# Four adaLN products per weight step kept side by side on TensorE, in the order 2, 3, 0, 1

## The chip, the cores and the metric

One core of a Trainium2 chip (trn2) runs the program. The metric is the device time of one execution in microseconds (us), and what is compared is the median of several executions.

## The reference, cut to what matters

One inference step of a two-layer backbone. 1024 sample tokens and 128 prompt tokens of width 1024 go through the same trunk: a convolutional mixer and a feed-forward in layer 0, attention and a feed-forward in layer 1. Each layer is steered by six vectors, computed from a conditioning vector, one for the samples and one for the prompt:

```
mod = silu(cond) @ ada_w[i] + ada_b[i]             # ada_w[i] is 1024 x 6144, cond 1 x 1024
sh1, sc1, g1, sh2, sc2, g2 = split(mod, 6)
h = modulate(rmsnorm(x, norm1_g[i]), sh1, sc1)
y = conformer_conv(h, ...)  or  gqa_mixer(h, ...)
x = x + g1 * y
h = modulate(rmsnorm(x, norm2_g[i]), sh2, sc2)
x = x + g2 * conv_ffn(h, ...)
```

`conformer_conv` is a product with 2 x 1024 columns, a gate `a * sigmoid(g)`, a depthwise convolution of 31 taps over the tokens, a layer norm, silu, and a product with 1024 columns.

## The kernel before

All 1152 tokens stay in SBUF with features on the partitions, in three chunks of 384 columns. Every large product is made of three (`mm3`, L245 to L249): weights and activations are split into a high and a low part, and high x high, high x low and low x high are summed. A weight tile of 128 x 1024 numbers is loaded by `Weights.load` (L209), split on ScalarE and VectorE (L220, L221) and handed out by `take`; loads run up to three tiles ahead.

The adaLN vectors come from `ada` (L252 to L303). A group is 2048 columns of `ada_w`; there are six groups, three for each layer. A group runs over the 1024 rows of `ada_w` in eight steps of 128 rows. For a step, `load` (L253) issues two transfers of 128 x 1024 numbers, half 0 and half 1 of the columns, each into a buffer of the tag `adaw`. The step then has four products (L270): the conditioning vectors (128 x 32, `cs`) against 512 columns each, products 0 and 1 on half 0, products 2 and 3 on half 1. Product q writes PSUM partitions 32q to 32q+31, so each of the four uses its own strip of 32 columns of TensorE. The next step's two loads are issued before this step's products stand in the program. After eight steps ScalarE copies the sums into a row that also takes an `adaw` buffer (L279), TensorE transposes it (L283), and VectorE adds the bias (L287).

The first group runs at the start, with seven `adaw` buffers. The other five run beside the convolution (L679): `ada` is a generator in the list `bg`, and every call of `tick` moves it by one step. For this the phase gives `adaw` three buffers (L633):

```
sC, slot_c = phase(adaw=(3, D), pacc=(2, CONV_N), tmp=(2, CONV_N))
```

The convolution's first product, `gated` (L572 to L600), goes over eight tiles j of 128 features. A tile takes two weight tiles, and for each of the three chunks computes `ppa` and `ppg`, 24 products of 384 columns each, so 144 products for a tile; then ScalarE takes the sigmoid (L594) and VectorE multiplies (L597). There are three ticks in a chunk, nine in a tile. With the taps behind it, VectorE does 19 (L658, L660) and GpSimd the rest (L651). Of the last tile, 16 taps are products with diagonals on TensorE (`dl`, L706); the mean of the layer norm is taken by products (`mu`, L722, L726). The layer norm and the product `pw2` follow.

What sets the order of the work. The whole program stands in `manual_schedule(engines={SP})`: the SP queue issues all these transfers in the order in which they are written, so weight loads and adaLN loads share one line. On the other engines the order is planned when the program is built (`schedule_with_timeline_sim=True`): the planner walks through its own estimate of time, and of the instructions whose inputs are there by that estimate the one written earliest goes first. The engines then run their lists in that order. A region under `manual_schedule(engines=ATT_ENGINES)`, which is TensorE alone, keeps the written order of its TensorE instructions; in the kernel before, only the attention of layer 1 is such a region.

Of the kernel before, what the change touches and what calls it, by code (L numbers as in the profile page):

```python
# [13 lines left out]
PSUM = bass.MemoryType.PSUM  # L14
# [4 lines left out]
KT = D // P  # L19
# [29 lines left out]
ATT_ENGINES = {mybir.EngineType.PE}  # L49
# [16 lines left out]


def pieces(c):
    """A chunk's columns by the conditioning of their tokens."""
    lo, hi = c * CH, (c + 1) * CH  # L70
    out = []
    if lo < NS:
        out.append((0, min(hi, NS) - lo, 0))
    if hi > NS:
        out.append((max(lo, NS) - lo, CH, 1))
    return out
# [3 lines left out]
def tile_hybrid_step(ctx: ExitStack, tc: tile.TileContext, a: dict, outs: list):  # L80
    nc = tc.nc
# [14 lines left out]
        return xp.tile([P, KT, CH], F32, tag="x", name=name)  # L96

    def phase(**slots):
        """SBUF of a phase: so many tiles of so many columns for each tag."""
        stack = ExitStack()  # L100
        pools = {
            tag: (stack.enter_context(tc.tile_pool(name=f"s_{tag}", bufs=bufs, reuse_waits="tile")), n)
            for tag, (bufs, n) in slots.items()
        }

        def tile_(tag, name, dt=F32, n=None):
            pool_, cols_ = pools[tag]
            return pool_.tile([P, n or cols_], dt, tag=tag, name=name)

        return stack, tile_  # L110
# [13 lines left out]
        return hh, hl  # L124

    class Banks:
        """PSUM, cut anew for some phases."""

        stack = None

# [12 lines left out]

    pool = Banks()

    # work that runs beside the products, a step after each of them
    bg = []

    def tick():
# [18 lines left out]

    xs_d = [dp.tile([P, NCH, KT, CH], F32, name=f"xs_d{i}") for i in range(2)]

    # ---- weights, in the order of their use: loads run up to three tiles ahead, the split into hi + lo (both exact
    # in float32r) one or two ----
    def ffn_order(l):
        up = a["ffn_w_up"][l]
        down_at = dict(DOWN)
# [23 lines left out]
    class Weights:  # L199
# [22 lines left out]
            self.ready[i] = tuple(t.rearrange("p (k n) -> p k n", n=n) if n else t for t in (hi, lo))  # L222

        def ahead(self, splits, loads):
            """Has everything up to so many tiles from the next one split or loaded."""
            for i in range(self.at, min(self.at + max(splits, loads), len(self.order))):
                if self.order[i][0] == "stop":
                    break
                if i < self.at + loads and i not in self.raw and i not in self.ready:
                    self.load(i)  # L230
                if i < self.at + splits and i not in self.ready:
                    self.split(i)
# [10 lines left out]
    weights = Weights()  # L243
# [4 lines left out]
        nc.tensor.matmul(ps, wh, ml, start=False, stop=False)  # L248
        nc.tensor.matmul(ps, wl, mh, start=False, stop=last)  # L249

# [1 line left out]
    def ada(pool, l, grp):  # L252
        def load(kt):  # L253
            out = []
            for half in range(2):
                w = slot("adaw", f"adaw{l}_{grp}_{kt}_{half}")
                c0 = grp * 2048 + half * 1024
                nc.sync.dma_start(w, a["ada_w"][l, kt * P : (kt + 1) * P, c0 : c0 + 1024])
                out.append(w)
            return out  # L260

        nxt = load(0)
        yield
        ps = pool("ms", f"ada{l}_{grp}")
        for kt in range(KT):
            w = nxt
            if kt + 1 < KT:
                nxt = load(kt + 1)
            for q in range(4):
                nc.tensor.matmul(  # L270
                    ps[32 * q : 32 * q + 32, :],
                    cs[:, kt, :],
                    w[q // 2][:, (q % 2) * 512 : (q % 2) * 512 + 512],
                    start=(kt == 0),
                    stop=(kt == KT - 1),
                )
            yield
        row = slot("adaw", f"adar{l}_{grp}", n=512)
        nc.scalar.activation(row, ps, AF.Copy)  # L279
        yield  # L280
        pt = pool("ms", f"adat{l}_{grp}")
        for i in range(4):
            nc.tensor.transpose(pt[:, i * P : (i + 1) * P], row[:, i * P : (i + 1) * P], ident)  # L283
        ptv = pt.rearrange("p (i q c) -> p q i c", i=4, c=32)
        b0 = grp * 16
        for cond in range(2):
            nc.vector.tensor_tensor(  # L287
                mods[l][:, b0 : b0 + 16, cond].rearrange("p (q i) -> p q i", i=4),
                ptv[:, :, :, cond],
                adab[:, l * 48 + b0 : l * 48 + b0 + 16].rearrange("p (q i) -> p q i", i=4),  # L290
                ALU.add,
            )
        for n, gname in ((0, "norm1_g"), (1, "norm2_g")):
            v = 1 + 3 * n
            if v // 2 == grp:
                for cond in range(2):
                    nc.vector.scalar_tensor_tensor(
                        gsc[l][n][:, :, cond],
                        mods[l][:, v * 8 : v * 8 + 8, cond],
                        1.0,  # L300
                        cols(gname, l * KT, KT),
                        ALU.add,
                        ALU.mult,  # L303
                    )
# [1 line left out]
    def mod(l, v, j, cond):  # L306
        return mods[l][:, v * 8 + j, cond : cond + 1]

# [1 line left out]
    def add_stat(acc, j, c, src, eng=None, tag=None):  # L310
        d = acc[:, c * CH : (c + 1) * CH]
        if j == 0:
# [4 lines left out]
            (eng or nc.gpsimd).tensor_tensor(d, d, sq, ALU.add)  # L317

    def token_rstd(pool, parts, name, bank=None):
        """Sums over features of all parts[f, token], then (mean + eps) ** -0.5, tokens on partitions."""  # L320
        n = CH // P
        ps = pool("ms", f"{name}_s") if bank is None else bank[:, CH:]
        for t in range(n):
            for i, x in enumerate(parts):
                nc.tensor.matmul(
                    ps[:, t : t + 1], x[:, t * P : (t + 1) * P], ones, start=(i == 0), stop=(i == len(parts) - 1)
                )
        return rstd_of(ps[:, 0:n], 1.0 / D, n, name)
# [6 lines left out]
        return rs  # L335

    def spread(pool, v, name, bank=None):
        """v[token, t] to every partition, tokens along the columns."""
        n = v.shape[1]
        ps = pool("ms", f"{name}_b") if bank is None else bank  # L340
        for t in range(n):
# [46 lines left out]
        nc.sync.dma_start(t, xs_d[i][:, c])  # L388
        return t

# [1 line left out]
    def ffn(pool, H, X, l, name, beside, done):  # L392
        acts = {}

# [83 lines left out]
        for g in gens:  # L478
            yield from g

    # =========================== layer 0 ===========================
    pool.open(mm=(4, 512), acc=(1, 1536), ms=(1, 512))

# [1 line left out]
    vec_rows = [  # L485
        ("c", a["c"].rearrange("b (r p) -> (b r) p", p=P)),
        ("c_ctx", a["c_ctx"].rearrange("(r p) -> r p", p=P)),
# [32 lines left out]
        nc.sync.dma_start(crow[at[name] : at[name] + KT, :], src)  # L520

    def load_x(c):
        """A chunk's tokens, on partitions, where the low parts of the normed chunks go later."""
        n = CH // P
        toks = hp.tile([P, n, D], F32, tag="hl", name=f"xt{c}")
        for t in range(n):
# [48 lines left out]
        pass  # L575
    weights.ahead(0, RING)

    # conformer: gated pointwise, depthwise over tokens, layernorm, silu, pointwise
    us = []

    def gated(j, c):
        """The products of a chunk; yields before their gating."""
        if c == 0:
            us.append((weights.take(min(j, 1)), weights.take(min(j, 1)), slot("u", f"u{j}")))
            for z in (0, NS + HALF, NT + 2 * HALF):
# [54 lines left out]
        return dww[:, j, t : t + 1]  # L640

    def taps_pool(j, u, pacc, t0, s0_, s1_):
        """The taps from t0 on, with the bias."""
        d = pacc[:, s0_:s1_]
        nc.scalar.activation(
            d, u[:, s0_ + t0 : s1_ + t0], AF.Identity, scale=tap(j, t0), bias=col("conv_dw_b", j)
# [4 lines left out]
            nc.gpsimd.tensor_tensor(d, d, tmp, ALU.add)  # L651

    def taps_vector(j, u, d, n, s0_, s1_, fresh):
        """The first n taps."""
        for t in range(n):
            src = u[:, s0_ + t : s1_ + t]
            if t == 0 and fresh:
# [31 lines left out]
        for c in range(NCH):  # L689
            join(j, da, pacc, c)  # L690

    # the last tile: some taps as products with diagonals, the others on top of them, chunk by chunk, so that the norm
    # of a chunk runs beside the taps of the next
    u = us[last][2]
    t0 = TAPS - POOL_TAPS_7
    te = t0 - PE_TAPS
# [107 lines left out]
    )  # L804
    H = H2

    # =========================== layer 1 ===========================
    # rotary tables with the norm gains folded in, tokens on partitions; gains: plain, halves swapped and signed
    NB = NS // P + 1
    sF.close()  # L810
    sK, slot = phase(s=(4 * NKV, SLOT))
# [55 lines left out]
            put_v(cv[:, kv * P : (kv + 1) * P], kv, NS // P)  # L867

    def head_norm(ps, which, tt, name):
        """RMS norm of two heads, rotary unless they are the prompt's; yields between its stages."""  # L870
        ss = tiny(f"{name}ss", 2)
        for h in range(2):
            nc.scalar.activation(
# [33 lines left out]
        yield xn  # L907

    def place(b, tt, o):
        """Heads to [feature, token]."""  # L910
        pt = pool("t", f"ptqk{b}_{tt}")
        for h in range(2):
            nc.tensor.transpose(pt[:, h * P : (h + 1) * P], o[:, h * P : (h + 1) * P], ident)
# [10 lines left out]
                AF.Copy,  # L924
            )

    # each slot: the products of a tile, then a further stage of each tile before it, the oldest first
    stages = []

    def advance():  # L930
# [46 lines left out]
    GRP = NH // NKV  # L977
    PC, PO = NCH - 1, NS - (NCH - 1) * CH

    # the prompt's queries see the prompt's own keys: the four heads of a group at once  # L980
    def prompt():
        for kv in range(NKV):
            q = qT[PC][:, kv * GRP : (kv + 1) * GRP, PO : PO + P]
# [50 lines left out]
            )  # L1034
            yield

    # samples: blocks of one head and the queries of one chunk, in steps of 128 queries; the scores run two steps
    # ahead of the transposes, the product with V one block behind them
    blocks = [(c, h) for c in range(NCH) for h in range(NH)]
    nq_of = lambda c: CH // P if c < PC else PO // P  # L1040
    steps = [(i, t) for i, (c, h) in enumerate(blocks) for t in range(nq_of(c))]
# [23 lines left out]
        st["ps"].append(ps)  # L1065

    def softmax(s, st):
        """Yields before each part of its exponential."""
        v = st["v"]
        nb, ls, ri = v[:, 3:4], v[:, 4:7], v[:, 7:8]  # L1070
        nc.vector.tensor_reduce(nb, v[:, 0:3], AX.X, ALU.max)
# [117 lines left out]
        project_residual(O, X, c, acc3, 1, "wo", "g")  # L1189
        bg.append(norm_mod(pool, X, acc3, c, 1, 1, H, "n3"))  # L1190

    # final norm, back to tokens on partitions
    gfs = []

    def final(acc, c):
# [40 lines left out]


def _rope_table():
    """cos and sin by position on the 64-wide grid: [128, 2, 9, 32]; block t < 8 is the row part of token tile t,
    block 8 the column part, which all tiles share."""  # L1240
    import numpy as np

    freqs = np.float32(10000.0) ** (-np.arange(0, 64, 2, dtype=np.float32) / np.float32(64))
# [32 lines left out]
```

## Time and profile before

| | before |
|---|---|
| median of 3 runs | 2789.68 us (2787.78 to 2792.02) |
| span of the profiled execution | 2789.3 us |
| PE busy | 2724.6 us, 98% of the span |
| DVE busy | 1585.4 us, 57% |
| ACT busy | 1053.5 us, 38% |
| POOL busy | 699.6 us, 25% |
| adaLN loads | 96 of 512 KB, 4.4 us from issue to landing in the median |

PE is TensorE, PEld its weight loads, DVE VectorE, ACT ScalarE, POOL GpSimd, SP the queue of SyncE that issues the transfers. A row of a timeline gives the start in us from the first instruction, how long the run of like instructions took, the engine, the line of the kernel, what it writes and reads, the shapes, how many instructions (x), and in brackets the idle time before it with what ended it. A product of two f32 operands is recorded as two instructions, so `x4` on an adaLN row is two products and `x8` is four; one with split operands (`ppa`, `ppg`) is one. The profiled execution's own time is told by its span alone; it lies within the three runs and 0.4 us under their median.

### The profile page before, as it was taken

The numbers are of one execution on the slowest core, as the hardware profiler recorded it, in microseconds if no ns is written. First come the engines' busy times: TensorE is split into PE (matmuls) and PEld (weight loads), VectorE is DVE, ScalarE is ACT, GpSimd is POOL, SyncE is SP. The second block draws the span as 40 slices with busy tenths as digits, with TensorE's granted clock in tenths as the row PEclk, the third lists the DMA queues.
The fourth block names the chain that finished last, engine by engine and source line by source line (L and its number), as shares of the span: only waits on it lengthen the run. The fifth ranks groups of instructions, "written<-read, shape, count | busy, mean of one in ns | idle before, by whom it ended". The sixth has DMA issues, their size and how long they took to land.

```text
span 2789.3 us, 40007 instructions
## 1 busy us (share of the span) xinstructions
PE 2724.6 (98%) x15959; PEld 2577.1 (92%) x15959; DVE 1585.4 (57%) x2743; ACT 1053.5 (38%) x2066; POOL 699.6 (25%) x782
## 2 busy tenths in 40 slices
PE   7999989999999999999999899999999999999999
PEld 4867649999999999999999799899999999999998
DVE  6878886544444444445643788766544444444445
ACT  5545546422222221222555777755422122221222
POOL 2777744300000000000555566535000000000003
PEclk9999989999999999999999999999999999999999
DMA  7465425311111111111210000044111111111111
GB/s 261 158 185 160 154 91 176 110 32 46 46 46 46 39 46 38 46 38 46 95 58 1 1 1 1 32 129 136 45 40 46 38 46 39 46 39 45 32 53 69
DMA packets 194419, 192.18 MB, mean 69 GB/s; under 512 B 7072, under 2 KB 173323, under 8 KB 192698
## 3 DMA queue, kind: packets, MB, share of 16 engines
q1 hardware_dynamic: 193946, 189.53, 21.7%
q8 instruction: 126, 2.06, 0.3%
q14 instruction: 59, 0.48, 0.1%
q0 software_dynamic: 288, 0.11, 0.0%
HBM read 175.19 MB, written 14.42 MB: 68 GB/s over the span
## 4 chain that ended last, share of the span: by engine, by line
PE 94%; DVE 3%; DMA 1%; ACT 1%; issue 0%; POOL 0%; SPq 0%; DVEq 0%; ACTq 0%; POOLq 0%
PE f1pd L249 3%; PE f1pd L247 3%; PE f1pd L248 3%; PE f1pg L249 3%; PE f0pg L249 3%; PE f1pg L248 3%; PE f0pg L248 3%; PE f0pv L247 3%; PE f0pg L247 3%; PE f1pv L249 3%; PE f1pg L247 3%; PE f0pv L248 3%; PE f1pv L248 3%; PE f1pv L247 3%; PE f0pv L249 3%; PE f0pd L248 3%
## 5 line engine op out<-in xcount | busy, mean ns | idle before, releaser
L220 ACT ACTIVATE w_hi<-w_raw 128x1024 fp32r<-128x1024 f32 x208 | 218.1, 1058 | 939.4 <-PE f0pd L248 223.7
L221 DVE TENSOR_TENSOR w_lo<-w_raw,w_hi 128x1024 fp32r<-128x1024 f32 x208 | 269.4, 1304 | 425.0 <-ACT w_hi L220 422.4
L651 POOL TENSOR_TENSOR pacc<-pacc,tmp 128x1167 f32<-128x1167 f32 (+2 forms) x98 | 234.2, 2393 | 64.8 <-ACT tmp L650 41.6
L384 DVE SCALAR_TENSOR_TENSOR x<-f1pd,mods,x 128x256 f32<-128x256 f32 (+1 forms) x352 | 170.2, 514 | 102.6 <-PE f1pd L249 102.4
L384 DVE SCALAR_TENSOR_TENSOR x<-f0pd,mods,x 128x256 f32<-128x256 f32 (+1 forms) x352 | 169.8, 514 | 99.1 <-PE f0pd L249 98.9
L660 DVE SCALAR_TENSOR_TENSOR da<-u,dww,da 128x1167 f32<-128x1167 f32 x126 | 180.8, 1435 | 2.8
L1084 POOL TENSOR_TENSOR pr<-pr,sm 128x384 f32<-128x384 f32 x192 | 153.8, 829 | 107.3 <-DVE sm L1082 49.4
L411 POOL MEMSET f1gp<- 128x1 f32 x66 | 3.7, 98 | 703.7 <-DVE f1gp L435 690.5
L411 POOL MEMSET f0gp<- 128x1 f32 x66 | 3.6, 98 | 703.8 <-DVE f0gp L435 690.7
L248 PE MATMUL f1pd<-f1al,w_hi 128*128 128x384 f32 x528 | 178.8, 339 | 0.0
L249 PE MATMUL f1pd<-f1ah,w_lo 128*128 128x384 f32 x528 | 178.7, 338 | 0.0
L249 PE MATMUL f0pd<-f0ah,w_lo 128*128 128x384 f32 x528 | 178.7, 338 | 0.0
L248 PE MATMUL f0pd<-f0al,w_hi 128*128 128x384 f32 x528 | 178.5, 338 | 0.0
L247 PE MATMUL f1pd<-f1ah,w_hi 128*128 128x384 f32 x528 | 178.5, 339 | 0.0
L247 PE MATMUL f0pd<-f0ah,w_hi 128*128 128x384 f32 x528 | 178.0, 338 | 0.0
L249 PE MATMUL f0pg<-n_h,w_lo 128*128 128x384 f32 x528 | 176.7, 335 | 0.0
L249 PE MATMUL f1pg<-n_h,w_lo 128*128 128x384 f32 x528 | 176.7, 335 | 0.0
L248 PE MATMUL f1pg<-n_l,w_hi 128*128 128x384 f32 x528 | 176.7, 335 | 0.0
L248 PE MATMUL f0pv<-n_l,w_hi 128*128 128x384 f32 x528 | 176.7, 335 | 0.0
L248 PE MATMUL f0pg<-n_l,w_hi 128*128 128x384 f32 x528 | 176.7, 335 | 0.0
L247 PE MATMUL f0pg<-n_h,w_hi 128*128 128x384 f32 x528 | 176.7, 335 | 0.0
L247 PE MATMUL f1pg<-n_h,w_hi 128*128 128x384 f32 x528 | 176.7, 335 | 0.0
(327 smaller groups left out, 7802.7 us busy)
## 6 DMA issues: line engine op xcount, KB each, us to landing
adaw<-in_ada_w_dram SPq DMA_DIRECT2D x96, 512.0 KB, 4.4
w_raw<-in_ffn_w_up_dram SPq DMA_DIRECT2D x88, 512.0 KB, 3.8
w_raw<-in_ffn_w_down_dram SPq DMA_DIRECT2D x44, 512.0 KB, 3.9
w_raw<-in_conv_w_pw_dram SPq DMA_DIRECT2D x40, 512.0 KB, 6.8
w_raw<-in_attn_w_o_dram SPq DMA_DIRECT2D x24, 512.0 KB, 4.4
xs_d<-x SPq DMA_DIRECT2D x6, 1536.0 KB, 11.1
x<-xs_d SPq DMA_DIRECT2D x6, 1536.0 KB, 7.8
w_raw<-in_attn_w_qkv_dram SPq DMA_DIRECT2D x12, 512.0 KB, 3.6
```

The lines of the kernel that those rows point to most:

```text
L220: nc.scalar.activation(hi, raw, AF.Copy)
L221: nc.vector.tensor_tensor(lo, raw, raw32(hi), ALU.subtract)
L247: nc.tensor.matmul(ps, wh, mh, start=first, stop=False)
L248: nc.tensor.matmul(ps, wh, ml, start=False, stop=False)
L249: nc.tensor.matmul(ps, wl, mh, start=False, stop=last)
L384: nc.vector.scalar_tensor_tensor(xx, ps[:, lo:hi], mod(l, v, j, cond), xx, ALU.mult, ALU.add)
L411: nc.gpsimd.memset(gp[:, z : z + 1], 0.0)
L651: nc.gpsimd.tensor_tensor(d, d, tmp, ALU.add)
L660: nc.vector.scalar_tensor_tensor(d, src, tap(j, t), d, ALU.mult, ALU.add)
L1084: nc.gpsimd.tensor_tensor(pr[n], pr[n], ri.to_broadcast([P, CH]), ALU.mult)
```

## The change

In `ada`, the four products of a step are put in a region in which TensorE keeps the written order, and half 1 is written ahead of half 0. Nothing else of the program's work changes; the rest of the diff takes out comments and docstrings.

```diff
-            for q in range(4):
-                nc.tensor.matmul(
-                    ps[32 * q : 32 * q + 32, :],
-                    cs[:, kt, :],
-                    w[q // 2][:, (q % 2) * 512 : (q % 2) * 512 + 512],
-                    start=(kt == 0),
-                    stop=(kt == KT - 1),
-                )
+
+            with tc.manual_schedule(engines=ATT_ENGINES):
+                for q in (2, 3, 0, 1):
+                    nc.tensor.matmul(
+                        ps[32 * q : 32 * q + 32, :],
+                        cs[:, kt, :],
+                        w[q // 2][:, (q % 2) * 512 : (q % 2) * 512 + 512],
+                        start=(kt == 0),
+                        stop=(kt == KT - 1),
+                    )
```

## Rows read from the trace of the kernel before

**Rows 1.** The page, part 4: the chain that ended last, by engine.
```profile
PE 94%; DVE 3%; DMA 1%; ACT 1%; issue 0%; POOL 0%; SPq 0%; DVEq 0%; ACTq 0%; POOLq 0%
```

**Rows 2.** Stretch 250 to 300 us: busy PE, PEld, DVE, ACT, POOL (instructions), clock, DMA.
```profile
250.00:300.00 50.00, 50.00 (x257) 35.63 (x255) 40.03 (x39) 24.07 (x23) 41.97 (x19) 1.00 0.58 175
```

**Rows 3.** PE timeline among the diagonal taps: start, duration, line, tiles, records.
```profile
336.74 1.07 PE L270 MATMUL ada<-adaw,cs 128*32 128x512 f32 x8
337.73 1.56 PE L706 MATMUL dl<-u,diag 128*128 128x384 f32 x4
339.22 1.05 PE L270 MATMUL ada<-adaw,cs 128*32 128x512 f32 x4
340.20 6.72 PE L706 MATMUL dl<-u,diag 128*128 128x384 f32 x20
346.86 1.05 PE L270 MATMUL ada<-adaw,cs 128*32 128x512 f32 x4
347.84 0.91 PE L706 MATMUL dl<-u,diag 128*128 128x384 f32 x2
348.68 1.05 PE L270 MATMUL ada<-adaw,cs 128*32 128x512 f32 x4
```

**Rows 4.** Instructions on tile ada, 110 to 395 us: duration min/median/max, first and last start.
```profile
L270 PE MATMUL ada<-adaw,cs x320: 592/593/618, 114.4 to 391.0; 128*32 128x512 f32 x160
```

**Rows 5.** PE timeline among the gated products, 130 to 140 us.
```profile
130.13 1.05 PE L270 MATMUL ada<-adaw,cs 128*32 128x512 f32 x4
...
133.07 1.05 PE L270 MATMUL ada<-adaw,cs 128*32 128x512 f32 x4
...
135.15 1.05 PE L270 MATMUL ada<-adaw,cs 128*32 128x512 f32 x4
...
136.41 0.34 PE L247 MATMUL ppg<-n_h,w_hi 128*128 128x384 f32 x1
...
138.85 0.34 PE L249 MATMUL ppg<-n_h,w_lo 128*128 128x384 f32 x1
...
139.12 1.05 PE L270 MATMUL ada<-adaw,cs 128*32 128x512 f32 x4
```

**Rows 6.** Waits of the SP queue, 110 to 395 us: total, times, longest.
```profile
SPq L258 <- PE ada L270: 185.6, 64, 7.2
```

**Rows 7.** DMA issues, 100 to 400 us: count, KB each, median us to landing.
```profile
adaw<-in_ada_w_dram SPq DMA_DIRECT2D x80, 512.0 KB, 4.3
w_raw<-in_conv_w_pw_dram SPq DMA_DIRECT2D x11, 512.0 KB, 6.9
```

**Rows 8.** SP timeline, 100 to 310 us: issue start, stretch, line, issues.
```profile
105.84 43.02 SPq L258 DMA_DIRECT2D adaw<-in_ada_w_dram  x16
...
201.85 1.48 SPq L209 DMA_DIRECT2D w_raw<-in_conv_w_pw_dram  x2
206.49 42.98 SPq L258 DMA_DIRECT2D adaw<-in_ada_w_dram  x14
...
297.59 1.05 SPq L209 DMA_DIRECT2D w_raw<-in_conv_w_pw_dram  x2
```

**Rows 9.** The chain in order of time, 294 to 313 us: start, duration, what.
```profile
297.59 6.92 DMA w_raw<-in_conv_w_pw_dram
...
304.54 1.06 ACT w_hi L220
...
306.71 0.32 PE ppa L249
```

**Rows 10.** Stretch 306 to 310 us, columns as in rows 2.
```profile
306.00:310.00 4.00, 4.00 (x16) 4.00 (x15) 4.00 (x3) 3.23 (x4) 3.10 (x2) 0.57 0.64 255
```

**Rows 11.** PE timeline, end of the convolution's products.
```profile
384.67 0.81 PE L726 MATMUL mu<-u,mean_w 128*128 128x384 f32 x2
```

**Rows 12.** SP timeline after the last adaLN load.
```profile
418.66 0.33 SPq L388 DMA_DIRECT2D x<-xs_d  x1
```

**Rows 13.** PE timeline of the first group, with the idle time before.
```profile
42.81 1.05 PE L270 MATMUL ada<-adaw,cs 128*32 128x512 f32 x4 [0.32 <-DMA adaw<-in_ada_w_dram]
```
## The prediction

> **What bounds the kernel now.** I read the page's chain first: TensorE carries 94% of it [rows 1]. So a TensorE instruction taken out of a stretch in which TensorE never rests is worth its time, if nothing else is nearly as late. The change touches the adaLN products alone, so I looked at the stretches that hold them. From 250 to 300 us TensorE is busy for all 50 us, VectorE for 40.0 and GpSimd for 42.0 [rows 2]: TensorE is the bound there, with 8 to 10 us in 50 to spare before another engine is. Next, the timeline of TensorE. Most adaLN rows are x4, half a step; a few are x8, a whole one [rows 3]. The 320 records between 114.4 and 391 us [rows 4] are 40 steps; counted in the timeline they stand in 71 blocks, parted by other products. Last, the SP queue: in those 285 us its adaLN loads waited 64 times, 185.6 us in all, for an adaLN product to give back its buffer [rows 6]. A load lands 4.3 us after its issue [rows 7]. This queue also carries the convolution's weights: between one pair of weight loads and the next stand some 14 adaLN loads, seven steps [rows 8]. So two things run side by side, TensorE's products and a ring of load, product, load over three buffers, and the second is almost as long as the first.
>
> **What joining takes away.** Records of the diagonal taps follow each other every 0.333 us (20 of them from 340.20 to 346.86). A half block there is followed by the next tap 0.98 us later, and the next two taps take 0.84 us in place of 0.67; a whole block is followed after 0.99 us, and its next four take 1.49 in place of 1.33 [rows 3]. So a block costs TensorE 1.15 us whether it holds two products or four: the strips work at the same time. If all 40 steps stand whole, 31 blocks go, 31 x 1.15 = 36 us of TensorE.
>
> **What waiting for the later half adds.** Half 0 used to give back its buffer as soon as it had landed and been used. Now half 0 is kept until half 1 is there, and both buffers come back together. Of three buffers, two hold the step and one holds the next step's half 0; the next half 1 has no buffer until the step is done. So every step now contains one whole load: 4.3 us of transfer [rows 7], the block, and some 0.1 us of signals, 5.5 us at least. Nothing prefetches the half that is waited for. Behind a block that waits stand the convolution's products on TensorE, whose list is fixed, and behind its loads the weights on SP; POOL's queue issues nothing in this stretch.
>
> Where other products stand under that load, TensorE loses nothing. How many the planner puts there can be read from before. A buffer used at 130.13 is used again three blocks later, at 139.12 [rows 5]; between them stand two other blocks and 31 products (5.6 us at 0.174 us each: 14 products from 136.41 to 138.85). On the chip the load is there after 4.3 us of those 7.9. The planner thus reckons with a load almost twice as long as it is, and puts the next block where it thinks that the load lands. In the new order no other blocks stand in that gap, so products take their place: two blocks are worth 2.3 / 0.174 = 13 products, so 44, or 37 if the first half of a block already gives back a buffer. I take 37. An interval so filled lasts 1.15 + 37 x 0.174 = 7.6 us.
>
> A tile of the convolution has 144 products, enough for 144 / 37 = 3.9 such intervals. Its nine ticks hold seven steps and most of one change of group, 7.9 intervals. The other 4.0 have no product to put in and last 5.5 us with TensorE idle for most of it: 3.9 x 7.6 + 4.0 x 5.5 = 51.6 us. Two things are added once in a tile. The weights that the queue reaches at the end of the tile's ticks take 6.9 us to land and 1.06 us to be split before a product can use them [rows 7, 9]; before, other work lay over that, now the block behind those products waits too: 6.9 + 1.06 - 4.3 = 3.7 us. And products that follow an idle stretch ran at half rate: after the wait of 297 to 305 us the next ones took 0.32 us each [rows 9], with the granted clock at 0.57 over 306 to 310 us, so between its two levels, 1.2 and 2.4 GHz [rows 10]; 12 products, 1.8 us. Together 57.1 us a tile.
>
> Before, four tiles of ticks lay between the first adaLN load at 105.84 and the weights of the last tile at 297.59 [rows 8], 47.9 us each. So +9.2 us a tile, **+37 us** until the last weights are issued.
>
> From there to the last `mu` product of the first chunk at 384.67 us [rows 11], before has 17 blocks. With a block only every 37 products or their worth (24 tap records take the place of 31 products between two uses of a buffer), 144 products and 110 records of `dl` and `mu` hold about 8. Nine fewer: **-10 us**. The three or four steps left over then fall under the layer norm, where TensorE waits for VectorE anyway; their loads stand on SP ahead of the reload of x, issued at 418.66 us [rows 12], so they have some 16 us of room, and cost one for one beyond that.
>
> In the first group seven buffers serve and TensorE already waits for the last half at 42.81 us [rows 13]. The refills start a half later: between 0 and +3 us, I take **+1**. Writing 2, 3 ahead of 0, 1 costs nothing by itself.
>
> The sum is 37 - 10 + 1 = +28 us. The profiled execution's span is 0.4 us under the median; I add to the median: 2789.7 + 28 = **2818 us**.
>
> **Bounds.** With 44 products in a filled interval a tile takes 59.8 us, +48 over four. Idle stretches may also put the blocks themselves at half rate, up to 1 us for each of 16 empty intervals, +16. With +3 at the start: 48 + 16 - 10 + 3 = +57, 2847 us. With neither the weights nor the clock felt: 3.7 x 4 - 10 = +5, 2795 us.
>
> The Trainium skill, "TensorE: Matmul & The Clock Gate", section "Loop structure matters more than you think", warns of a loop that waits for a transfer between its matmuls: they then run at the low clock. Rows 10 agree for one such wait; by the page alone the +16 us would be certain and the sum 2834 us.
>
> **Rivals.**
> *The products spread evenly* (faster). If the planner spreads the 144 products over all intervals, 18 in each (3.2 us), they lie under the 4.3 us of every load and 7.9 x 5.5 = 43.5 us make a tile. The weights then have cover: -4.4 a tile, -18 over four, and -10 at the end, **2762 us**. It decides at 25 products in an interval ((5.5 - 1.15) / 0.174): while no interval holds more, joining wins. For it: GpSimd and VectorE, at 42 and 40 of 50 us [rows 2], would just allow it. Against it: blocks were put in the middle of a product's sums, so adaLN goes first and products are used up as fast as they come [rows 5]. 12%.
> *Joining alone counts* (faster). If loads keep ahead in some way that I don't see, the 36 us are the result: **2754 us**. For it: a whole block costs as little as a half [rows 3]. Against it: 64 waits for buffers already [rows 6]. 5%. The Trainium skill, "TensorEngine Tiling (Array Packing)", section "Key Properties", says that such strips work independently and in parallel; rows 3 agree.
> *Gain and loss cancel*, or the planner parts the four after all and little changes: **2790 us**. With fewer than two empty intervals in a tile the loss is no more than the gain. 9%.
> *TensorE keeps the written order around each block too* (slower). Then the 24 products of each `ppa` and `ppg` stand between two blocks and lie under the load, 43.5 us a tile as above; but none can go ahead, so the weights come bare, 6.9 + 1.06 us, and one batch of 24 products behind them, 4.2 us. That is 55.7 us a tile, +31 over four, with nothing won at the end: **2821 us**. 6%.
>
> **How the numbers follow.** The forecast has 68%; with the last rival, slower by over 0.2% (5.6 us, about what a measurement of this kernel can tell from no change) has 74%. The two fast rivals give 17% to faster, the third 9% to the same. The range reaches from 2782, which takes in the middle of the cases and small gains, to 2847; the faster rivals' own values lie below it.
>
> **What would show it.** Right: adaLN rows of TensorE are x8 throughout, 40 blocks; intervals fall into two kinds, some 7.6 us or more with about 37 products and some 5.5 us with next to none; TensorE's busy share between 110 and 400 us falls from full to some 80%, ended by the landing of `adaw`; the pairs of weight loads stand some 57 us apart on SP, not 48; pieces of that stretch show a lower clock. After the layer norm every stage only starts later. Wrong: pairs of weight loads no more than 48 us apart, or TensorE still fully busy there. If the intervals are right but products run at the full clock, the term of 1.8 us is off; if the last group ends far behind 418 us, the room that I gave it was not there.

## The result, and the profile after

The changed kernel took 2806.1 us (median of four runs, 2804.96 to 2807.09) against 2789.3 us before (2787.78 to 2792.02): a ratio of 1.0059, 95% interval 1.0045 to 1.0074, so some 16.5 us slower. The forecast was 2818. The profiled execution of after has a span of 2805.1 us and took 2806.85 itself.

The page of after, the row of busy times and the chain by engine (which answers to [rows 1]):

```profile
PE 2698.0 (96%) x15959; PEld 2580.7 (92%) x15959; DVE 1589.6 (57%) x2743; ACT 1054.6 (38%) x2066; POOL 705.4 (25%) x782
...
PE 92%; DVE 3%; DMA 3%; ACT 1%; issue 1%; POOL 1%; SPq 0%; DVEq 0%; POOLq 0%; ACTq 0%
```

Read this against the small table of before. TensorE's busy time fell by 26.6 us (2724.6 to 2698.0) with the same 15959 instructions: joining did take work from it. But the span grew by 15.8, so TensorE's idle time rose by 42.4 us, from 64.7 to 107.1. DMA's part of the chain went from 1% to 3%. The question is only where TensorE now stands still.

The stretches of after; the first answers to [rows 2], columns as there:

```profile
250.00:300.00 50.00, 37.39 (x198) 28.34 (x197) 38.97 (x38) 19.30 (x20) 35.54 (x16) 0.80 0.54 168
110.00:400.00 290.00, 255.91 (x1326) 188.76 (x1324) 235.45 (x225) 136.06 (x151) 218.50 (x107) 0.91 0.51 160
```

The same long stretch of before:

```profile
110.00:400.00 290.00, 284.73 (x1337) 185.87 (x1336) 235.35 (x234) 137.98 (x155) 215.86 (x109) 0.99 0.53 162
```

TensorE was busy for 284.7 of 290 us and is now busy for 255.9; from 250 to 300 us it is busy for 37.4 of 50, and the granted clock of that stretch is 0.80 in place of 1.00. VectorE and GpSimd have become hardly later: over the 290 us their busy times are within 3 us of those of before.

The tile view of `ada` in after, 110 to 400 us (answers to [rows 4]), and the waits of the same instructions, 100 to 400 us (total, times, longest):

```profile
L272 PE MATMUL ada<-adaw,cs x304: 592/617/1062, 118.2 to 397.0; 128*32 128x512 f32 x152
```

```profile
PEld ada L272 <- DMA adaw<-in_ada_w_dram: 41.1, 9, 6.6
PE ada L272 <- DMA adaw<-in_ada_w_dram: 31.2, 8, 4.8
```

In before a record of an adaLN product (two make a product) took 593 ns in the median and 618 at most. Now the maximum is 1062. The first row of waits is that of TensorE's weight loads, nine times and 41.1 us, and one of the nine lasts only 0.25 us. The second is that of the products: eight times a block stands still for its load, 31.2 us in all. The timeline of TensorE shows where (it answers to [rows 5]; first some steps beside many products, then the end of a tile):

```profile
124.45 1.06 PE L272 MATMUL ada<-adaw,cs 128*32 128x512 f32 x8
130.70 1.07 PE L272 MATMUL ada<-adaw,cs 128*32 128x512 f32 x8
...
248.37 1.06 PE L272 MATMUL ada<-adaw,cs 128*32 128x512 f32 x8
253.64 1.93 PE L272 MATMUL ada<-adaw,cs 128*32 128x512 f32 x8 [2.24 <-DMA adaw<-in_ada_w_dram]
...
266.92 1.94 PE L272 MATMUL ada<-adaw,cs 128*32 128x512 f32 x8 [4.76 <-DMA adaw<-in_ada_w_dram]
269.81 0.69 PE L247 MATMUL ppg<-n_h,w_hi 128*128 128x384 f32 x1 [0.96 <-ACT w_hi L220]
```

Every row is x8, a whole step. There are two kinds of intervals. In the first, blocks stand 6.25 us apart with 29 products between them, TensorE never waits, and the load is hidden. In the second nothing is left to stand between two blocks: 4.7 us of waiting and a block of 1.93 us, 6.6 us together. Where the first kind passes into the second, one interval holds the last 2 to 10 products of the tile and a shorter wait (2.24 us at 253.64). The chain of waits of after, in order of time, shows the same and what follows (answers to [rows 9]):

```profile
249.46 4.13 DMA adaw<-in_ada_w_dram
253.64 1.96 PE ada L272 x8
255.60 4.59 DMA adaw<-in_ada_w_dram
260.23 2.01 PE ada L272 x8
...
262.57 6.11 DMA w_raw<-in_conv_w_pw_dram
268.71 1.07 ACT w_hi L220
269.81 0.69 PE ppg L247
...
270.82 0.32 PE ppa L247
```

Load, block, load, block; then the weights for 6.11 us and their split for 1.07, with nothing over them but one more block, the one at 266.92. A product that comes behind takes 0.32 us in place of 0.17 until 274 us, so nearly twice as long; the granted clock from 269.81 to 274.00 us is 0.50, the lower of TensorE's two levels, 1.2 GHz. From 253.64 to 262.00, where the blocks take 1.93 us in place of 1.06, it is 0.50 too.

The SP queue of after (answers to [rows 8]):

```profile
108.67 48.47 SPq L258 DMA_DIRECT2D adaw<-in_ada_w_dram  x16
157.19 1.05 SPq L209 DMA_DIRECT2D w_raw<-in_conv_w_pw_dram  x2
...
212.49 1.05 SPq L209 DMA_DIRECT2D w_raw<-in_conv_w_pw_dram  x2
...
262.57 1.05 SPq L209 DMA_DIRECT2D w_raw<-in_conv_w_pw_dram  x2
...
313.74 1.05 SPq L209 DMA_DIRECT2D w_raw<-in_conv_w_pw_dram  x2
...
381.13 22.09 SPq L258 DMA_DIRECT2D adaw<-in_ada_w_dram  x6
435.28 0.33 SPq L390 DMA_DIRECT2D x<-xs_d  x1
```

From the first adaLN load to the weights of the last tile are now 205.1 us, before 191.8: 51.3 us a tile, not 47.9. TensorE in these two stretches, after and then before, columns as in [rows 2]:

```profile
108.67:313.74 205.07, 176.35 (x996) 139.20 (x994) 182.80 (x162) 102.88 (x96) 178.84 (x79) 0.90 0.54 170
105.84:297.59 191.75, 191.75 (x973) 134.39 (x972) 157.09 (x147) 95.44 (x91) 157.95 (x73) 1.00 0.59 180
```

Its busy time fell by 15.4 us, although a part of it now runs at the lower level; its idle time rose from nothing to 28.7 us. That is the loss: 13.3 us.

And the first load itself comes at 108.67 us, 2.8 later than before. That has another cause, at the start. The chain of before, 52 to 54 us:

```profile
52.36 1.28 DVE n_l L364
...
53.69 0.69 PE ppa L248
```

The timeline of TensorE there in after:

```profile
49.88 0.69 PE L247 MATMUL ppa<-n_h,w_hi 128*128 128x384 f32 x1 [4.31 <-ACT n_h L365]
50.37 0.52 PE L247 MATMUL ppg<-n_h,w_hi 128*128 128x384 f32 x1
56.79 1.02 PE L624 MATMUL pvec<-ident,rows 31*128 31x31 f32 x8 [5.90 <-DMA rows<-in_conv_dw_w_dram]
57.75 0.69 PE L248 MATMUL ppa<-n_l,w_hi 128*128 128x384 f32 x1
```

And the same `pvec` in before:

```profile
80.10 0.68 PE L622 MATMUL pvec<-ident,rows 31*128 31x31 f32 x8
```

`pvec` turns the taps of the depthwise convolution; the rows that it turns are loaded into a buffer of the same tag `adaw` as the first group's weights. In before the planner put it at 80 us, behind many products. In after it stands behind the first two products and waits 5.9 us for its transfer, with the whole convolution queued behind it: the products with `n_l` begin at 57.75 us, not 53.69. The loss is less than the 5.9 us because in before these products had to wait too, for `n_l` on VectorE.

### The profile page after: what moved, and what is told of

Its sections match the earlier page's. It is cut to its first block, busy times and chain, and to the rows that moved or that the text cites. A ratio compares the mean times of both kernels' runs of the same rounds, so it can differ in the third digit from the quotient of the medians.

```text
span 2805.1 us, 40000 instructions
## 1 busy us (share of the span) xinstructions
PE 2698.0 (96%) x15959; PEld 2580.7 (92%) x15959; DVE 1589.6 (57%) x2743; ACT 1054.6 (38%) x2066; POOL 705.4 (25%) x782
## 4 chain that ended last, share of the span: by engine, by line
PE 92%; DVE 3%; DMA 3%; ACT 1%; issue 1%; POOL 1%; SPq 0%; DVEq 0%; POOLq 0%; ACTq 0%
PE f1pd L249 3%; PE f1pd L247 3%; PE f1pd L248 3%; PE f1pg L249 3%; PE f0pg L249 3%; PE f0pg L248 3%; PE f1pv L247 3%; PE f1pg L248 3%; PE f1pg L247 3%; PE f0pv L247 3%; PE f0pg L247 3%; PE f0pv L248 3%; PE f1pv L249 3%; PE f0pv L249 3%; PE f1pv L248 3%; PE f0pd L248 3%
## 5 line engine op out<-in xcount | busy, mean ns | idle before, releaser
L653 POOL TENSOR_TENSOR pacc<-pacc,tmp 128x1167 f32<-128x1167 f32 (+2 forms) x98 | 237.2, 2424 | 51.3 <-ACT tmp L652 45.3
L1086 POOL TENSOR_TENSOR pr<-pr,sm 128x384 f32<-128x384 f32 x192 | 154.0, 831 | 107.1 <-DVE sm L1084 55.4
```

Source lines behind the costliest of these rows:

```text
L1086: nc.gpsimd.tensor_tensor(pr[n], pr[n], ri.to_broadcast([P, CH]), ALU.mult)
```

## The experiments

Each kernel ran beside runs of the kernel before on the same chip. Theory P is the one of the prediction: loads kept until the later half is there, so that a step contains one whole load.

**1. A fourth buffer.** If the ring of three buffers is the loss, one more buffer, which lets the next step's second half be loaded ahead, must turn it into the gain of joining. One `u` buffer less makes the room.

```diff
-    sA, slot_a = phase(... u=(3, NT + 3 * HALF))
+    sA, slot_a = phase(... u=(2, NT + 3 * HALF))
...
-    sC, slot_c = phase(adaw=(3, D), ...
+    sC, slot_c = phase(adaw=(4, D), ...
```

> The changed kernel with four adaw buffers beside the convolution in place of three, so that both halves of the next step can be loaded ahead; the room comes from u, two buffers for three. Theory P (with three buffers every joined step contains one whole load): the idle intervals go, TensorE is busy again between 110 and 390 us, and the 31 blocks saved show, 2754 to 2775 us. Rival J (a joined block costs by itself, through its four strips or its fixed order): still slower than before, 2795 us or more.

Measured: 2761.9 us, ratio 0.9901 (0.9887 to 0.9916), 44 us faster than after with the same order of products. Its stretches, columns as in [rows 2], and its blocks on TensorE:

```profile
110.00:300.00 190.00, 190.00 (x1139) 148.40 (x1137) 183.34 (x161) 110.50 (x116) 179.47 (x78) 1.00 0.75 246
300.00:360.00 60.00, 51.47 (x183) 31.43 (x182) 59.41 (x67) 27.00 (x37) 42.67 (x32) 0.91 0.04 14
```

```profile
206.32 1.07 PE L272 MATMUL ada<-adaw,cs 128*32 128x512 f32 x8
210.84 1.07 PE L272 MATMUL ada<-adaw,cs 128*32 128x512 f32 x8
214.84 1.07 PE L272 MATMUL ada<-adaw,cs 128*32 128x512 f32 x8
```

Blocks now come some 4 us apart in the middle of a group (4.5 and 4.0 here) with 13 to 19 products between them; at its ends 3 to 30 stand there. No block waits, and TensorE is busy for every one of the 190 us at the full clock (1.00, 2.4 GHz). VectorE with 183 and GpSimd with 179 of 190 us are nearly as late, and from 300 us on VectorE (59.41 of 60) sets the pace. Theory P stands.

**2. The smaller `u` alone.** Only the `u` lines of the diff above.

> The control for the four buffers: the changed kernel with two buffers for u and three adaw buffers as it was. Theory P: within 6 us of the changed kernel, 2800 to 2812 us, idle intervals as there. Rival U (what the four buffers gain comes from u): moves toward the time with four buffers.

Measured: 2806.3 us, ratio 1.0061 (1.0046 to 1.0076). What four buffers win does not come from `u`.

**3. Four buffers without joining.** The kernel before with the diff of experiment 1.

> The kernel before with four adaw buffers and two for u: loads run further ahead, pairs stay parted. Theory P: little to win, since TensorE was busy throughout and the number of blocks hardly falls, 2780 to 2795 us. Rival J: the same. Rival B (buffers alone are what counts, joined or not): as fast as the changed kernel with four buffers, 2754 to 2775 us.

Measured: 2785.9 us, ratio 0.9985 (0.9976 to 0.9994), TensorE busy for 283.93 of 290 us from 110 to 400 us. Halves that stay parted need the fourth buffer little: 4 us. Joining needs it, and is worth 0.9985 - 0.9901, so 23 us, once it has it. (With four buffers both kernels have the smaller `u`.)

**4. The order without the region.** Is it the kept order that joins the four, or half 1 ahead of half 0?

```diff
-            for q in range(4):
+            for q in (2, 3, 0, 1):
```

> The kernel before with the halves in the order 2, 3, 0, 1 and no region of kept order. Theory S (the order of the halves alone joins the four: when half 1 is there, half 0 is there too): as the changed kernel, 2800 to 2812 us, all adaLN rows x8. Rival M (the region holds them together): as before, 2784 to 2795 us, rows x4.

Measured: 2805.7 us, ratio 1.006 (1.0043 to 1.0077), and in the timeline all 40 steps whole, as in after. The order of the halves does all of it.

**5. The region without the order.** The reverse:

```diff
+            with tc.manual_schedule(engines=ATT_ENGINES):
+                for q in range(4):
```

> The change without its new order: the four products of a step stand in a kept-order region on TensorE, but as 0, 1, 2, 3, half 0 first. Theory R (the region ties the four together, whatever their order): blocks are whole, x8, and the time is that of after, 2800 to 2812 us. Theory O (only the order of the halves joins them; the region fixes the order among the four and lets other products between): blocks are mostly x4, some 70 of them between 110 and 400 us, TensorE is busy throughout, and the time is that of before, 2784 to 2795 us.

Measured: 2790.8 us, ratio 1.0009 (0.9999 to 1.0018). In the timeline the 40 steps stand in 71 blocks, as in before, and from 250 to 300 us TensorE is busy for all 50 us. A region that keeps the order of four instructions does not keep them together: other products are planned between them.

**6. The loads swapped as well.** After, with half 1 loaded ahead of half 0:

```diff
-            out = []
-            for half in range(2):
+            out = [None, None]
+            for half in (1, 0):
...
-                out.append(w)
+                out[half] = w
```

> After, with the two loads of a step issued the other way round as well, half 1 first and half 0 last; products still 2, 3, 0, 1. Now the half that is used first also lands first, as before. Theory O (what counts is that the half that lands last is used first, so that both buffers are kept until then): blocks are parted again, x4, no empty interval, and the time is that of before, 2784 to 2795 us. Rival (the order 2, 3, 0, 1 costs something by itself, by the strips that it uses or by the region): 2800 to 2812 us.

Measured: 2793.8 us, ratio 1.0016 (1.0007 to 1.0025); 75 blocks, TensorE busy for 288.8 of the 290 us from 110 to 400, no empty interval. So it is not 2, 3, 0, 1 by itself, but the half that lands last going first. What is left, 4.5 us (2 to 7), I had not expected. In its trace `pvec` stands early and waits 5.74 us for its rows, as in after, so a loss at the start like that of experiment 7 would fit.

**7 and 8. The first group and the others apart.** The change under a condition, for the first group alone and for the other five alone:

```diff
+            if (l, grp) == (0, 0):
...
+            if (l, grp) != (0, 0):
```

> The change in the first group alone, the one at the start with seven buffers; the five groups beside the convolution as before. My term for this group was +1 us (0 to 3). Theory: 2787 to 2794 us, the rest as before, with the first adaLN load of the second group within 3 us of its place before. Rival (the start pays for a good part of the loss, since everything waits for the first group): 2796 us or more.

Measured: 2792.2 us, ratio 1.0009 (0.9999 to 1.0018). TensorE's timeline:

```profile
57.29 1.03 PE L631 MATMUL pvec<-ident,rows 31*128 31x31 f32 x8 [5.79 <-DMA rows<-in_conv_dw_w_dram]
```

> The change in the five later groups alone; the first group as before. Theory (the loss comes from the three buffers beside the convolution): 2800 to 2808 us, some 51 us between pairs of weight loads. Rival (the start pays for a good part): 2795 us or less.

Measured: 2798.8 us, ratio 1.0036 (1.0022 to 1.0051), a little below what I expected. TensorE's timeline:

```profile
79.41 0.67 PE L631 MATMUL pvec<-ident,rows 31*128 31x31 f32 x8
```

The early `pvec` comes with the new order in the first group. The five later groups cost 10 us (6 to 14): 51.0 us between pairs of weight loads, and from 110 to 400 us TensorE waits for `adaw` seven times, in after eight. The first group alone costs 2.5 us (0 to 5). The two sums give 12.5 of the 16.5 us; the intervals leave room for the rest, and in the first group's trace the product of [rows 11] begins only 1.2 us late (385.87), though the first `n_l` product is 4.6 us late. So parted steps may swallow a part of a late start that joined ones pass on; that was not tried by itself.

**9. The rows loaded early.** After with two `u` buffers (experiment 2), and the rows that `pvec` turns loaded at the start by GpSimd's queue, in buffers of their own (the edit that makes these buffers is left out here):

```diff
+    rows = slot("rows", "rows0")
+    nc.gpsimd.dma_start(rows[0:TAPS, :], a["conv_dw_w"][0])
+    frow = slot("frow", "rows1")
+    for l in range(2):
+        nc.gpsimd.dma_start(
...
-    rows = slot("adaw", "rows0")
-    nc.sync.dma_start(rows[0:TAPS, :], a["conv_dw_w"][0])
...
```

> After with two u buffers, and with the rows that pvec turns (the taps of both convolutions) loaded at the start into buffers of their own, by POOL's queue; pvec stands as early on TensorE as in after, but its data is there. Without these loads the same kernel took 2806.3 us. Theory (the wait for rows is the first group's loss): no wait before pvec, first convolution products 4 us earlier, 2800 to 2804 us. Rival (swallowed later, or another cause at the start): 2805 to 2809 us.

Measured: 2799.2 us, ratio 1.0034 (1.0021 to 1.0047), 7 us less than with the late rows and just under the range that I gave. TensorE's timeline:

```profile
50.14 1.03 PE L624 MATMUL pvec<-ident,rows 31*128 31x31 f32 x8 [1.67 <-issue]
...
55.78 0.69 PE L248 MATMUL ppa<-n_l,w_hi 128*128 128x384 f32 x1 [0.21 <-DVE n_l L366]
```

`pvec` stands as early as in after, and no longer waits for a transfer. But at the first `n_l` product only 1.7 us of the 7 are there (55.78 against 57.44 in experiment 2), not the 4 that I expected: in this run the first group's last load came later, so that its last block begins at 43.77 us and not at 41.17, and the product then waits for `n_l` on VectorE. Of the rest some 3 us lie in the four tiles, whose plan changed a little too. So the run shows that the wait can be removed, and is not a clean price for it.

**10. The best of both.** Four buffers, two `u`, joined steps in the five later groups, the first group as before (experiments 1 and 8 together).

> The change in the five later groups alone, the first group in the order of before, with four adaw buffers and two u buffers. Theory (what the change costs in the first group is the wait of the eight pvec products for the transfer of rows, which the planner then puts ahead of the first convolution products; it comes on top of the rest): the run with the change everywhere and four buffers took 2762 us, this one 2754 to 2760 us, pvec rows far behind the first products and no wait of 5 to 6 us before them. Rival (the first group's wait is swallowed later by waits for the weights): 2760 to 2765 us.

Measured: 2753.3 us, ratio 0.987 (0.9857 to 0.9884): 37 us faster than before, just under the range that I gave, and below experiment 1, whose interval begins where this one's ends. The product that [rows 11] shows begins at 350.02 us here and at 355.10 in experiment 1. These two differ in the first group alone, as do experiment 8 (394.03) and after (398.89). Both pairs price the new order of the first group, with its early `pvec`, at 5 us there, and at 6 to 9 us by the times.

**11. Two buffers, joined.**

```diff
-    sC, slot_c = phase(adaw=(3, D), ...
+    sC, slot_c = phase(adaw=(2, D), ...
```

> After with two adaw buffers in place of three. Theory (the loss is the load that a step must wait for, because its buffers come back together): now both halves are loaded after the block, nothing is ahead, and an empty interval lasts longer than the 6.6 us of after; 38 products stand in a filled one by the plan. 2815 to 2850 us. Rival (the third buffer does not help joined steps): 2803 to 2810 us.

Measured: 2840.0 us, ratio 1.018 (1.0166 to 1.0194). TensorE's timeline:

```profile
118.68 1.07 PE L272 MATMUL ada<-adaw,cs 128*32 128x512 f32 x8
126.49 1.07 PE L272 MATMUL ada<-adaw,cs 128*32 128x512 f32 x8
...
224.05 1.93 PE L272 MATMUL ada<-adaw,cs 128*32 128x512 f32 x8 [5.23 <-DMA adaw<-in_ada_w_dram]
231.22 1.94 PE L272 MATMUL ada<-adaw,cs 128*32 128x512 f32 x8 [5.24 <-DMA adaw<-in_ada_w_dram]
```

Filled intervals of 7.8 us with 38 products, empty ones of 7.2. With one buffer less both grow, and the time with them. Experiments 11, after and 1 are one series, two, three and four buffers: 2840, 2806, 2762 us.

**12. Two buffers, parted.** The same edit on the kernel before.

> Before with two adaw buffers in place of three: halves parted, each buffer back as soon as its half is used. Theory: a step then has to hold one whole load as in after, but two half blocks per step instead of one whole, and products between them; the plan has some intervals of 6 and some of 28 products. 2800 to 2830 us. Rival (parted halves need no third buffer): 2786 to 2794 us.

Measured: 2842.7 us, ratio 1.0189 (1.0173 to 1.0204), slower than both ranges that I gave. The timeline of TensorE:

```profile
218.14 1.92 PE L270 MATMUL ada<-adaw,cs 128*32 128x512 f32 x4 [1.81 <-DMA adaw<-in_ada_w_dram]
220.95 1.92 PE L270 MATMUL ada<-adaw,cs 128*32 128x512 f32 x4 [0.89 <-DMA adaw<-in_ada_w_dram]
```

Here each half block waits for its own load, and runs at the lower level: 1.92 us for a half, as much as for a whole one. With two buffers parted steps lose as much as joined ones; with three they are within 4 us of four (experiment 3), and from 105.84 to 297.59 us TensorE never stands still. That room is what after gave away.

## Why the prediction was right, and where its sizes were off

**Direction and mechanism: right.** All 40 steps stand whole. The intervals fall into the two kinds that were forecast, TensorE's busy share from 110 to 400 us falls to 88% (forecast "some 80%"), ended by the landing of `adaw`, and the clock is lower there. The two fast rivals did not come: the plan put 29 products into an interval, more than the 25 at which the prediction sets the border between gain and loss. Whether the border lies at 25 no run tests, since with three buffers the joined order had this one plan; that experiment 1 comes out at the first rival's 2762 us is chance, as it gets there by a fourth buffer. The rival that TensorE keeps the written order around each block did not come, and experiment 5 shows the region doing nothing at all.

**The four tiles: +37 forecast, +13.3 measured** (205.1 - 191.8). The step that was mis-sized is "I take 37". The plan put 29 products in a filled interval. With 29 the prediction's own formula gives 144 / 29 = 5.0 filled intervals of 6.2 us and 2.9 empty ones of 5.5, 46.9 us; with its 5.5 us for weights and clock 52.4 us a tile, so +18 over four in place of +37. I had let the two blocks that used to stand in the gap be replaced by products, because they take TensorE 2.3 us. But between two uses of a buffer there were 31 products before and there are 29 now, with the blocks gone: they seem to weigh next to nothing in the planner's estimate. That is read from the two traces, not from a run made for it. For the remaining 5 us: the first tile has no empty interval at all, so that in the four tiles TensorE waits for `adaw` seven times in place of 16, 26.4 us in all. The bare weights cost less than the 3.7 us that I gave them: TensorE stands idle for 0.96 us in front of the first product (269.81), because their load and split run beside the block that waits. This happens twice in the four tiles, not four times: the first pair of weights, at 157.19, brings no wait, and the wait behind the last pair falls in the next term. Against that, an empty interval lasts 6.6 us, not 5.5, mostly because its block runs at the lower level. That was the upper bound's term, +16 us for 16 blocks; the eight blocks up to 318 us that ran there took 0.87 us more each, 7 in all. The Trainium skill, "TensorE: Matmul & The Clock Gate", section "Loop structure matters more than you think", says that with a long wait for a transfer in front of every matmul TensorE goes cold and the matmul runs at the low clock. The rows of 1.93 us behind waits of 2.2 to 4.8 us agree. Not every single wait did it: in experiment 11 a block behind a wait of 3.29 us, at 277.40, took 1.07 us.

**From the last weights on: -10 forecast, -1.9 measured** (313.74 to 398.89 against 297.59 to 384.67). The nine blocks did go: 88 records in 18 blocks before (the prediction has 17), 72 in nine after. But the stretch begins with an empty interval and bare weights. The stretch and TensorE's timeline in after:

```profile
313.74:398.89 85.15, 79.77 (x335) 50.33 (x336) 53.68 (x63) 33.37 (x55) 40.99 (x28) 0.93 0.45 137
```

```profile
318.16 1.93 PE L272 MATMUL ada<-adaw,cs 128*32 128x512 f32 x8 [4.82 <-DMA adaw<-in_ada_w_dram]
321.05 0.69 PE L247 MATMUL ppg<-n_h,w_hi 128*128 128x384 f32 x1 [0.96 <-ACT w_hi L220]
```

The same stretch of before:

```profile
297.59:384.67 87.08, 83.65 (x337) 47.64 (x336) 72.01 (x76) 39.81 (x61) 59.00 (x35) 0.98 0.49 153
```

TensorE is idle for 5.4 us, 2 more than before, and the clock of 0.93 against 0.98 is worth, as an estimate, some 4 us more of 80. These two make 6 of the 8 us; the rest is open. I had counted four such stalls in the tiles; one of them belongs here.

**The first group: +1 forecast, 2.8 us measured at the first adaLN load, and 5 us or more later on** (experiments 8 and 10; experiment 7, the first group by itself, shows 2.5, 0 to 5). The term that I looked at, the refills of seven buffers, does not show: the group's last products end at 43.0 us, before at 43.9 [rows 13]. What I missed is that the planner, given another order in one place, moved `pvec` forward, in front of the products that everything waits for. Why it did so is not shown; that its rows take an `adaw` buffer, as the first group's loads do, may be the link. The prediction named no row of `pvec`.

**The room behind the layer norm** was there: the last adaLN loads are issued by 403.2 us and the reload of x follows at 435.28, 16.6 us later than in [rows 12], as the whole stage has moved. The sum of the measured terms is 2.8 + 13.3 - 1.9 = 14.2 us at the first chunk's `mu`; in the span of the whole execution it is 15.8. That the forecast came within 12 us is partly luck: the term of the tiles was 24 us too high, and the gain behind them 8 us too high as well, which took a third of that back.

## What to carry to other kernels

Count the buffers of a ring against what stands between its consumers: the operand that lands last, used first, keeps all the earlier ones until then, and a ring that was just deep enough becomes one load too short. If such a join saves engine time, give it a buffer more before judging it: here the same join lost 16.5 us with three buffers and took 23 us off with four, each against parted steps with as many. And where a planner orders the instructions, look for what else moved, ahead of the first work that everything waits for.

## What the runs showed that I had not expected

- A kept-order region around four products joined nothing (2790.8 us, 71 blocks), and the order of the halves without it did everything (2805.7 us).
- A half block and a whole one take the same at the lower level too, 1.92 and 1.93 us, as 1.05 and 1.06 at the full one.
- Parted halves are no safer than joined ones when the ring is short: 2842.7 and 2840.0 us with two buffers.
- With the join and four buffers TensorE loses its place as the only bound: VectorE is busy for 183 of 190 us beside it, and for 59.4 of 60 us behind it.
